# Reordering the expert matmuls by term, and moving result copies, stores, the final norm and the opening, in a two-layer backbone on one core

## The chip, the cores and the metric

The kernel runs on one NeuronCore of a Trainium2 chip. The metric is device time in microseconds (us) of one execution; the value shown is the median of 3 runs.

## The reference

A two-layer diffusion backbone over 256 latent tokens and 256 context tokens, model width 1024. The part that the change touches is the start of layer 0 (a modulated norm) and the expert part of layer 1:

```python
h_lat = modulate(rms_norm(x, norm_g[layer, 0]), sh_m, sc_m)      # shift and scale from silu(c) @ ada_w + ada_b
...
def moe_swiglu(h, w_router, b_router, w_gate, w_up, w_down):
    logits = (h @ w_router + b_router).astype(jnp.float32)
    top_v, top_i = lax.top_k(logits, TOP_K)                      # 2 of 8 experts
    weights = jax.nn.softmax(top_v, axis=-1)
    ...
    for e in range(N_EXPERTS):
        y = y + combine[..., e:e + 1] * swiglu(h, w_gate[e], w_up[e], w_down[e])   # 1024 -> 3584 -> 1024
...
return rms_norm(x, final_g)
```

## The kernel before

**Split products.** Every large product is made in three matmuls. A float32 operand is split into a high part (rounded) and a low part (the rest). `mm3` (L218) then issues high x high (L219), high x low or low x high (L220, L221) into the same accumulator. Weights come from memory as blocks of 128 x 2048 float32, 1 MB each: SP's queue loads a block (`load`, L164), ScalarE makes the high part `wh` (L181), VectorE the low part `wl` (L182). `unit` hands the next split block to TensorE and sends ahead up to 8 loads and, from the first expert on, 4 splits. The order of the blocks is a list (`_sequence`).

**Queues.** Each engine executes its instructions in order; a layer below the kernel decides the order in which an engine's instructions stand, and adds the waits. DMAs issued by SP and ScalarE share eight completion slots in rotation: an issue waits until the earlier DMA of its slot has landed.

**Opening.** x is loaded in four parts, and its squares are summed (`stats_add`, ScalarE and VectorE). TensorE sums over partitions (L359). VectorE takes the inverse root in nine short steps (`rsqrt`, L340 to L351), and TensorE spreads it by four transposes (L388). The modulation is a product of silu(c) with ada_w. Its first columns come in four groups (`ada_first(q)`, L314), each of two 1 MB blocks, 16 matmuls a block, which show as 32 pieces or fewer in a trace row. ScalarE copies the group (L317), TensorE transposes it (L319), VectorE adds the bias. Then x is multiplied (L434) and modulated (`affine_split`, L406 to L408), and the first projection starts (L219 to L221, `mm<-wh,hx`).

**Experts.** 8 experts, each at most 128 token slots, in 7 chunks of 512 hidden columns. A chunk has six units (weight blocks): two of the gate `mg`, two of up `mu`, two of down `md` for the chunk before. `half` (L1066) issues 12 matmuls for a gate or up block, accumulators `mm`; `expert_out` (L1094) issues 12 for a down block, into two accumulators `ys` (`pss`), one for each half of the output columns. `turn` (L1087) transposes the chunk's hidden values (L1090) and splits them (`ahi` by ScalarE, `alo` by VectorE). After the last chunk of experts 0 to 6, `keep_rows` copies both accumulators to buffers `yh` and `yl` on ScalarE (L1135) and stores them to `yrow` from ScalarE's queue (L1136). In the last expert the weights of the final norm, `fg`, are loaded into the same two buffers (L1246), rows of `yrow` are gathered by POOL (L1175), and `combine` (L1183) weighs and adds them on VectorE, spread over TensorE's steps (`background`).

**End.** The last expert's output is scattered (L1124, L1126), `norm_parts` squares and sums (L1273) and multiplies by the norm's weights. Then every engine reads the largest slot count and branches (L1280, L1281): the block behind it, for experts with more than 128 tokens, is not entered with these inputs. Behind the branch stand the final inverse root (L1299, `rsqrt`), the scaling (L1304, L1306) and the four stores (L1307).

Of the kernel before, what the change touches and what calls it, by code (L numbers as in the profile page):

```python
# [29 lines left out]
LOADX = 8  # L30
WIDTHS = (4, 2, 4, 4, 4, 4)
LEAD = 3
NA_ORDER = (4, 3, 0, 1, 2)
NA_FILL = (0, 0, 2, 2, 2, 2, 2, 2, 2, 2)
FFN_FILL = (3, 3, 3, 3, 2, 2)
# [76 lines left out]
def _program(tc, A, out):  # L112
# [32 lines left out]
    def small(shape, dt=F32, tag="sm", bufs=4):  # L145
        pool = smallp if tag in ("rs_v", "rs_y", "rs_t", "fss", "fs2") else wp
        return pool.tile(shape, dt, tag=tag, name=nm(tag), bufs=bufs)
# [70 lines left out]
    def mm3(ps, lh, ll, rh, rl, start, stop):  # L218
        pe.matmul(ps, lhsT=lh, rhs=rh, start=start, stop=False)  # L219
        pe.matmul(ps, lhsT=lh, rhs=rl, start=False, stop=False)  # L220
        pe.matmul(ps, lhsT=ll, rhs=rh, start=False, stop=stop)  # L221

    def put_split(hi, lo, src):
        return (act.activation(hi, src, AF.Copy),  # L224
# [129 lines left out]
    def stats_begin(nk, nt):  # L354
        return {"nk": nk, "nt": nt, "acc": None, "ps": None}
# [26 lines left out]
    def stats_end(st, d, rs=None):  # L382
        nt = st["nt"]
        if rs is None:
            rs = stats_rstd(st, d)
        bc = ps_s()
        for tt in range(nt):
            pe.transpose(bc[:, tt * P:tt * P + P], rs[:, tt:tt + 1].to_broadcast([P, P]), ident)  # L388
        return bc
# [26 lines left out]
                                     ALU.mult, ALU.add)  # L416


    st = stats_begin(KD, 4)
    for k in range(KD):  # L420
        stats_add(st, x[:, k, :], k)
    ada_first(0, ps_mm)
    bc = stats_end(st, 1024)

    gp = newpool("gp", 1)
    tn = gp.tile([P, 2, 4, 512], F32, tag="ug", name="tn")
# [631 lines left out]
    def step():  # L1058
        if background and next(background[0], True):
            background.pop(0)  # L1060
# [5 lines left out]
    def half(e, c, name, xg, ps, tag):  # L1066
        for h in range(2):
            wh, wl = unit(name, e, c, h, *tag)
            for kk in range(4):
                k = 4 * h + kk  # L1070
                mm3(ps, xg[:, k, 0, :], xg[:, k, 1, :], wh[:, 512 * kk:512 * kk + 512],
                    wl[:, 512 * kk:512 * kk + 512], k == 0, k == 7)
                if kk % SP == SP - 1:
                    step()

    def expert_in(e, c, xg, mid, *tag):
        pg = ps_mm()
        half(e, c, "mg", xg, pg, tag)
        a = mop.tile([P, 512], F32, tag="a", name=nm("a"))
        act.activation(a, pg, AF.Silu)  # L1080
        mid()
        pu = ps_mm()
        half(e, c, "mu", xg, pu, tag)
        last_mult[0] = vec.tensor_tensor(a, a, pu, ALU.mult)
        return a

    def turn(stt):  # L1087
# [7 lines left out]
    def expert_out(e, c, stt, ys, *tag):  # L1095
        last = e == NE - 1 and c == NCH - 1 and not tag
        for h in range(2):
            wh, wl = unit("md", e, c, h, *tag)
            jn = [(j, n) for j in range(2) for n in range(2)]
            jn.sort(key=lambda t: t[1])  # L1100
            for j, n in jn:
                f = 2 * h + j
                w0 = 1024 * j + 512 * n
                mm3(ys[n], stt["hi"][:, f * P:f * P + P], stt["lo"][:, f * P:f * P + P], wh[:, w0:w0 + 512],
                    wl[:, w0:w0 + 512], c == 0 and f == 0, c == NCH - 1 and f == 3)

    def slots_T(S):
        pt = ps_t()
# [23 lines left out]
    def keep_rows(e, ys):  # L1132
        for n in range(2):
            yv = mop.tile([P, 512], F32, tag=("yh", "yl")[n], name=nm("yv"), bufs=1)
            act.activation(yv, ys[n], AF.Copy)  # L1135
            nc.scalar.dma_start(yrow[e * P:e * P + P, 512 * n:512 * n + 512], yv)  # L1136

    def row_numbers():
        sm = lambda t, w=8: mop1.tile([P, 2, w] if w > 1 else [P, 2], F32, tag=t, name=nm(t))
# [36 lines left out]
                                         bass.IndirectOffsetOnAxis(ap=ri[:, 0:1], axis=0))  # L1176

    fetched = []
    last_mult = [None]

    def combine(tt):
        yy = fetched[tt]
        for n in range(2):  # L1183
            h_ = slice(512 * n, 512 * n + 512)
            a, b = yy[:, 0, h_], yy[:, 1, h_]
            with tc.issue_after(last_mult[0].ins):
                vec.tensor_scalar(a, a, rows[0][1][:, tt:tt + 1], None, ALU.mult)
            vec.scalar_tensor_tensor(a, b, rows[1][1][:, tt:tt + 1], a, ALU.mult, ALU.add)
            yield
            vec.tensor_tensor(a, a, gf[:, h_], ALU.mult)  # L1190
            vec.tensor_tensor(acc[:, tt, h_], acc[:, tt, h_], a, ALU.add)
            yield
# [78 lines left out]
    def norm_parts():  # L1271
        for n, tt, h_ in halves:
            act.activation(ps_t(), acc[:, tt, h_], AF.Square, accum_out=ss[:, tt, n:n + 1])  # L1273
            if n == 0:
                vec.tensor_tensor(o[:, tt, h_], acc[:, tt, h_], fg[n], ALU.mult)

    norm_parts()


    nmax = nc.values_load(cnt[0:1, 8:9], min_val=0, max_val=2 * P)  # L1280
    with tc.If(nmax > P):  # L1281
        for e in range(NE):
            n_e = nc.values_load(cnt[0:1, e:e + 1], min_val=0, max_val=2 * P)
            with tc.If(n_e > P):
                po2 = mop1.tile([P, 2, 8], F32, tag="po2", name=nm("po2"))
                vec.tensor_scalar(po2, pos, -float(P), None, ALU.add)
                xo, so, g = gather(po2, e)
                drain(g)
                ys = [ps_s(), ps_s()]
                for c in range(NCH):  # L1290
                    stt = {"a": expert_in(e, c, xo, lambda: None, "o")}
                    turn(stt)
                    expert_out(e, c, stt, ys, "o")
                scatter_now(e, ys, slots_T(so[0]))
        norm_parts()


    s2 = small([P, 2], tag="fs2", bufs=1)
    vec.tensor_tensor(s2, ss[:, :, 0], ss[:, :, 1], ALU.add)  # L1299
    rs = rsqrt(s2, 2, 1.0 / 1024)  # L1300
    for n, tt, h_ in halves:
        r = rs[:, tt:tt + 1]
        if n == 0:
            act.activation(o[:, tt, h_], o[:, tt, h_], AF.Identity, scale=r)  # L1304
        else:
            vec.scalar_tensor_tensor(o[:, tt, h_], acc[:, tt, h_], r, fg[n], ALU.mult, ALU.mult)  # L1306
        (nc.sync if n else nc.scalar).dma_start(out[0, tt * P:tt * P + P, h_], o[:, tt, h_])  # L1307
    xrp.release()
    mop.release()
    mop1.release()  # L1310
# [130 lines left out]
```

## Time and profile before

| | |
|---|---|
| median of 3 runs | 1835.57 us (1835.47 to 1837.29) |
| the profiled execution's own time | 1834.27 us |
| its span, first to last instruction | 1832.2 us |
| TensorE busy (PE) | 1773.5 us, 97% |
| VectorE busy (DVE) | 1332.0 us, 73% |
| ScalarE busy (ACT) | 1012.3 us, 55% |
| mean granted TensorE clock | 0.991 |
| read from memory | 476.13 MB, 263 GB/s over the span |

PE is TensorE's matmul row, PEld its weight loads (beside it), POOL is GpSimd, SP the load queue. A matmul's time in a row includes its way through the array, so the spacing of starts tells the stream's speed. "q" behind an engine marks its queue's DMA issues.

### The profile page before, as it was taken

The page shows a single profiled execution, that of the slowest core. Times are in us where ns is not written, and L with a number is a line of the kernel's source. Part 1 is how long each engine was busy: PE and PEld are TensorE (multiplying, and loading weights), DVE is VectorE, ACT ScalarE, POOL GpSimd, SP SyncE. Part 2 cuts the span into 40 slices and gives each one's busy share as a digit, 9 for nine tenths or more (in the row PEclk, how much of TensorE's full clock was granted, in tenths as well). Part 3 has the DMA queues.
Part 4 walks back from the last instruction along what each step waited for, and adds up shares of the span by engine and source line. Part 5 has one row for each costly group of instructions (what it writes and reads, how often), then busy time and mean ns, then how long its engine had stood idle before and what let it go on. Part 6 is the DMA issues. An engine that isn't in the chain of part 4 may idle for free. (4 is left out here: it accounts for less than half of the span.)

```text
span 1832.2 us, 21637 instructions
## 1 busy us (share of the span) xinstructions
PE 1773.5 (97%) x8548; PEld 1408.9 (77%) x8548; DVE 1332.0 (73%) x1413; ACT 1012.3 (55%) x1031; POOL 20.4 (1%) x19
## 2 busy tenths in 40 slices
PE   6999998999999999999999999999999999999996
PEld 4775477888888878588888878878878788788774
DVE  5632745564455578758988888888888888888797
ACT  3323634232222245746777766766766767776664
POOL 0000000000000000000000000000000000000010
PEclk9999998999999999999999999999999999999998
DMA  9567321464254317037999979989989899898990
GB/s 367 186 231 266 133 97 58 149 207 140 101 196 138 124 58 218 24 139 279 380 403 369 392 290 397 397 318 419 385 332 419 313 404 396 321 418 330 365 414 26
DMA packets 72606, 485.49 MB, mean 265 GB/s; under 512 B 7984, under 2 KB 8624, under 8 KB 16944
## 3 DMA queue, kind: packets, MB, share of 16 engines
q1 hardware_dynamic: 66416, 469.27, 66.4%
q10 hardware_dynamic: 4176, 7.94, 1.2%
q0 software_dynamic: 1904, 6.82, 1.0%
q8 instruction: 69, 1.13, 0.3%
q14 instruction: 41, 0.34, 0.0%
HBM read 476.13 MB, written 5.77 MB: 263 GB/s over the span
## 5 line engine op out<-in xcount | busy, mean ns | idle before, releaser
L182 DVE TENSOR_TENSOR wl<-raw,wh 128x2048 fp32r<-128x2048 f32 (+1 forms) x461 | 899.3, 1983 | 221.9 <-ACT wh L181 220.3
L181 ACT ACTIVATE wh<-raw 128x2048 fp32r<-128x2048 f32 (+1 forms) x461 | 745.5, 1664 | 304.6 <-PE mm L220 166.8
L220 PE MATMUL mm<-wl,xg 128*128 128x512 f32 x896 | 353.4, 394 | 11.9 <-DVE wl L182 11.9
L219 PE MATMUL mm<-wh,xg 128*128 128x512 f32 x896 | 350.6, 391 | 0.0
L221 PE MATMUL mm<-wh,xg 128*128 128x512 f32 x896 | 349.1, 390 | 0.0
L220 PEld LDWEIGHTS mm<-wl,xg 128*128 128x128 f32 x896 | 168.3, 188 | 53.9 <-DVE wl L182 20.7
L219 PEld LDWEIGHTS mm<-wh,xg 128*128 128x128 f32 x896 | 168.2, 188 | 35.1
L219 PE MATMUL mm<-hx,wh 128*128 128x512 f32 (+1 forms) x496 | 191.3, 390 | 3.8 <-ACT hx L406 3.8
L221 PEld LDWEIGHTS mm<-wh,xg 128*128 128x128 f32 x896 | 168.3, 188 | 33.8
L220 PE MATMUL mm<-hx,wh 128*128 128x512 f32 (+1 forms) x496 | 192.1, 387 | 0.0
L221 PE MATMUL mm<-hx,wl 128*128 128x512 f32 (+1 forms) x496 | 191.9, 387 | 0.0
L220 PE MATMUL pss<-wl,ahi 128*128 128x512 f32 x448 | 179.6, 401 | 2.7 <-DVE wl L182 2.7
L221 PE MATMUL pss<-wh,alo 128*128 128x512 f32 x448 | 175.2, 392 | 0.3 <-DVE alo L225 0.3
L219 PE MATMUL pss<-wh,ahi 128*128 128x512 f32 x448 | 161.4, 392 | 1.4 <-ACT wh L181 0.7
L219 PEld LDWEIGHTS mm<-hx,wh 128*128 128x128 f32 x496 | 94.0, 190 | 26.2 <-ACT hx L406 4.5
L220 PEld LDWEIGHTS mm<-hx,wh 128*128 128x128 f32 x496 | 94.3, 190 | 18.8
L221 PEld LDWEIGHTS mm<-hx,wl 128*128 128x128 f32 x496 | 94.0, 190 | 18.7
L224 ACT ACTIVATE ahi<-pst 128x512 fp32r<-128x512 f32 x56 | 33.4, 597 | 130.8 <-PE pst L1090 130.8
L220 PEld LDWEIGHTS pss<-wl,ahi 128*128 128x128 f32 x448 | 84.6, 189 | 20.1 <-DVE wl L182 4.0
L219 PEld LDWEIGHTS pss<-wh,ahi 128*128 128x128 f32 x448 | 84.2, 188 | 19.8 <-ACT wh L181 1.1
L221 PEld LDWEIGHTS pss<-wh,alo 128*128 128x128 f32 x448 | 84.7, 189 | 17.1 <-DVE alo L225 0.7
L415 DVE SCALAR_TENSOR_TENSOR x<-mm,mod,x 128x256 f32<-128x256 f32 x120 | 52.0, 478 | 39.4 <-PE mm L221 39.4
(305 smaller groups left out, 1893.6 us busy)
## 6 DMA issues: line engine op xcount, KB each, us to landing
raw<-in_mg SPq DMA_DIRECT2D x112, 1024.0 KB, 7.8
raw<-in_mu SPq DMA_DIRECT2D x112, 1024.0 KB, 8.3
raw<-in_md SPq DMA_DIRECT2D x112, 1024.0 KB, 7.9
raw<-in_ada SPq DMA_DIRECT2D x48, 1024.0 KB, 5.7
raw<-in_na_in SPq DMA_DIRECT2D x10, 1024.0 KB, 5.2
raw<-in_fg SPq DMA_DIRECT2D x10, 1024.0 KB, 5.0
raw<-in_fu SPq DMA_DIRECT2D x10, 1024.0 KB, 4.9
raw<-in_fd SPq DMA_DIRECT2D x10, 1024.0 KB, 5.0
```

The costliest lines, as they stand in the source:

```text
L181: act.activation(h_, r_, AF.Copy)
L182: vec.tensor_tensor(l_, r_, h_.bitcast(F32), ALU.subtract)
L219: pe.matmul(ps, lhsT=lh, rhs=rh, start=start, stop=False)
L220: pe.matmul(ps, lhsT=lh, rhs=rl, start=False, stop=False)
L221: pe.matmul(ps, lhsT=ll, rhs=rh, start=False, stop=stop)
L224: return (act.activation(hi, src, AF.Copy), vec.tensor_tensor(lo, src, hi.bitcast(F32), ALU.subtract))
L415: vec.scalar_tensor_tensor(x[:, db, a:b], ps[:, a:b], mod[:, l, g0 + db, c:c + 1], x[:, db, a:b], ALU.mult, ALU.add)
```

## The change

- `half` and `expert_out` issue their matmuls term by term over a block: in `half` four high x high, four with the tokens' low part, then four with the weights' low part; in `expert_out` high x high, weights' low part, hidden values' low part, for both output halves together. The last block of the program keeps the output halves apart.
- `keep_rows`: the second copy goes to VectorE, both stores to POOL's queue.
- `combine`: its first multiplication goes from VectorE to ScalarE, behind the latest Silu.
- The final norm, with its stores, becomes `final_norm`, called ahead of the branch, and again inside it.
- Opening: 30 matmuls of `ones` by `ones` come first; the spreading transposes of the inverse root are issued behind the first modulation group.

```diff
+WARM = 30
...
+    def mm3_by_term(jobs, order):
+        for i_, term in enumerate(order):
+            for ps, lh, ll, rh, rl, start, stop in jobs:
+                l_, r_ = {"hh": (lh, rh), "lh": (ll, rh), "hl": (lh, rl)}[term]
+                pe.matmul(ps, lhsT=l_, rhs=r_, start=start and i_ == 0, stop=stop and i_ == 2)
...
+    warm = ps_t()
+    for _ in range(WARM):
+        pe.matmul(warm[:, 0:P], lhsT=ones, rhs=ones, start=True, stop=True)
     st = stats_begin(KD, 4)
...
-    ada_first(0, ps_mm)
-    bc = stats_end(st, 1024)
...
+    first_stats()
+    last = ada_first(0, ps_mm)
+    rs = stats_rstd(st, 1024)
+    with tc.issue_after(last.ins):
+        bc = stats_end(st, 1024, rs)
...
-            for kk in range(4):
-                k = 4 * h + kk
-                mm3(ps, xg[:, k, 0, :], xg[:, k, 1, :], wh[:, 512 * kk:512 * kk + 512],
-                    wl[:, 512 * kk:512 * kk + 512], k == 0, k == 7)
-                if kk % SP == SP - 1:
-                    step()
+            mm3_by_term([(ps, xg[:, k, 0, :], xg[:, k, 1, :], wh[:, 512 * (k % 4):512 * (k % 4) + 512],
+                          wl[:, 512 * (k % 4):512 * (k % 4) + 512], k == 0, k == 7) for k in range(4 * h, 4 * h + 4)],
+                        ("hh", "lh", "hl"))
+            step()
...
+            if last and h == 1:
+                for n in range(2):
+                    mm3_by_term([t for t, (_, n_) in zip(jobs, jn) if n_ == n], ("hh", "hl", "lh"))
+            else:
+                mm3_by_term(jobs, ("hh", "hl", "lh"))
...
-            act.activation(yv, ys[n], AF.Copy)
-            nc.scalar.dma_start(yrow[e * P:e * P + P, 512 * n:512 * n + 512], yv)
+            if n:
+                vec.tensor_copy(yv, ys[n])
+            else:
+                act.activation(yv, ys[n], AF.Copy)
+            nc.gpsimd.dma_start(yrow[e * P:e * P + P, 512 * n:512 * n + 512], yv)
...
-            with tc.issue_after(last_mult[0].ins):
-                vec.tensor_scalar(a, a, rows[0][1][:, tt:tt + 1], None, ALU.mult)
+            with tc.issue_after(last_silu[0].ins):
+                act.activation(a, a, AF.Identity, scale=rows[0][1][:, tt:tt + 1])
...
     norm_parts()
+    final_norm()
```

TensorE's order at the start of the program, before (`raw_94`, `raw_96` are the two blocks of the first modulation group, `raw_100`, `raw_102` those of the second, `mm_237` the first projection):

```order
L359 MATMUL pss_143<-ones,w_141 128x1 x4
L388 MATMUL pss_205<-c_ident,rs_y_195 128x128
L314 MATMUL mm_152<-raw_94,c_cond 32x128 x16
L388 MATMUL pss_205<-c_ident,rs_y_195 128x128 x3
L314 MATMUL mm_152<-raw_96,c_cond 32x128 x16
L319 MATMUL pst_189<-c_ident,w_187 128x128
L314 MATMUL pss_249<-raw_100,c_cond 32x128 x16
L314 MATMUL pss_249<-raw_102,c_cond 32x128 x16
L219 MATMUL mm_237<-wh_243,hx_214 128x512
```

and now:

```order
L428 MATMUL pst_120<-ones 128x128 x30
L366 MATMUL pss_174<-ones,sacc_153 128x1 x4
L366 MATMUL pss_174<-ones,w_172 128x1 x4
L321 MATMUL mm_183<-raw_94,c_cond 32x128 x16
L321 MATMUL mm_183<-raw_96,c_cond 32x128 x16
L395 MATMUL pss_236<-c_ident,rs_y_226 128x128 x4
L326 MATMUL pst_220<-c_ident,w_218 128x128
L321 MATMUL pss_280<-raw_100,c_cond 32x128 x16
L321 MATMUL pss_280<-raw_102,c_cond 32x128 x16
L220 MATMUL mm_268<-wh_274,hx_245 128x512
```

The first group's products stand ahead of the spreading transposes; the second group's stand ahead of the first projection matmul, as before.

TensorE's order from the end of expert 6's last down block (`pss_...9`, `pss_...0` its two accumulators) into the next units, now:

```order
L228 MATMUL pss_12010<-wl_12734,ahi_12726 128x512
L228 MATMUL pss_12009<-wh_12733,alo_12727 128x512
L228 MATMUL pss_12010<-wh_12733,alo_12727 128x512
L228 MATMUL pss_12009<-wh_12733,alo_12727 128x512
L228 MATMUL pss_12010<-wh_12733,alo_12727 128x512
L228 MATMUL mm_12817<-wh_12751,xg_12169 128x512 x8
L228 MATMUL mm_12817<-wl_12752,xg_12169 128x512 x4
L228 MATMUL mm_12817<-wh_12770,xg_12169 128x512 x8
L228 MATMUL mm_12817<-wl_12771,xg_12169 128x512 x4
```

The low weights `wl` are read by the last four of a unit's twelve matmuls, and the two accumulators of a down block are finished one matmul apart.

ScalarE's order at the same place, before (`yv` the result copies, `yrow` their stores, `fg` the final norm's weights, `a` the Silu):

```order
L1135 ACTIVATE yv_12773<-pss_11978 128x512
L1136 DMA yrow<-yv_12773 128x512
L181 ACTIVATE wh_12739<-raw_12652 128x2048
L1135 ACTIVATE yv_12776<-pss_11979 128x512
L1246 DMA fg_13167<-in_fg_row 128x512
L181 ACTIVATE wh_12757<-raw_12670 128x2048
L1136 DMA yrow<-yv_12776 128x512
L181 ACTIVATE wh_12789<-raw_12700 128x2048
L1080 ACTIVATE a_12823<-mm_12786 128x512
L1246 DMA fg_13168<-in_fg_row 128x512
L181 ACTIVATE wh_12807<-raw_12718 128x2048
```

and now:

```order
L1157 ACTIVATE yv_12804<-pss_12009 128x512
L182 ACTIVATE wh_12770<-raw_12683 128x2048
L1268 DMA fg_13198<-in_fg_row 128x512
L182 ACTIVATE wh_12788<-raw_12701 128x2048
L1268 DMA fg_13199<-in_fg_row 128x512
L1094 ACTIVATE a_12854<-mm_12817 128x512
L182 ACTIVATE wh_12820<-raw_12731 128x2048
```

One copy and both stores are gone from this queue, and both loads of `fg` stand earlier; each of them waits for the store out of the buffer that it fills.

## Rows read from the trace of the kernel before

**Rows 1.** Busy by stretch (us): PE, PEld, DVE, ACT, POOL; granted clock; DMA share; GB/s.

```profile
100.00:150.00 50.00, 50.00 (x253) 37.18 (x252) 18.08 (x25) 12.24 (x16) 0.00 (x0) 1.00 0.60 219
1200.00:1250.00 50.00, 48.69 (x221) 39.57 (x220) 41.72 (x27) 34.48 (x26) 0.94 (x1) 1.00 0.84 336
1700.00:1750.00 50.00, 44.99 (x190) 35.02 (x190) 41.92 (x28) 33.83 (x23) 3.40 (x3) 0.97 1.01 409
```

**Rows 2.** Timeline, expert boundary at 1213 us, PE: start, us, what, [idle before <-releaser].

```profile
1213.30 0.39 PE L219 MATMUL mm<-wh,xg 128*128 128x512 f32 x1
1216.02 0.39 PE L219 MATMUL mm<-wh,xg 128*128 128x512 f32 x1
1217.71 0.50 PE L220 MATMUL mm<-wl,xg 128*128 128x512 f32 x1 [1.31 <-DVE wl L182]
```

**Rows 3.** Timeline, the same boundary, ACT and DVE.

```profile
1212.36 0.60 ACT L1135 ACTIVATE yv<-pss 128x512 f32<-128x512 f32 x1 [0.57 <-PE pss L221]
1213.42 1.92 ACT L181 ACTIVATE wh<-raw 128x2048 fp32r<-128x2048 f32 x1 [0.46 <-DVE alo L225]
1215.37 2.29 DVE L182 TENSOR_TENSOR wl<-raw,wh 128x2048 fp32r<-128x2048 f32 x1 [2.09 <-ACT wh L181]
```

**Rows 4.** Waits view, window 975 to 1700: total us, times, longest.

```profile
PE mm L220 <- DVE wl L182: 6.8, 5, 1.6
```

**Rows 5.** Waits view, window 1735 to 1802.

```profile
PE mm L220 <- DVE wl L182: 2.9, 6, 0.6
```

**Rows 6.** Timeline, last expert, ACT and PE.

```profile
1700.04 0.39 PE L219 MATMUL mm<-wh,xg 128*128 128x512 f32 x1
1708.25 0.36 ACTq L1246 DMA_DIRECT2D fg<-in_fg_row  x1
1708.71 5.51 ACT L181 ACTIVATE wh<-raw 128x2048 fp32r<-128x2048 f32 x3 [3.55 <-DMA yrow<-yv]
1709.58 0.39 PE L221 MATMUL mm<-wh,xg 128*128 128x512 f32 x1
1713.00 0.80 PE L220 MATMUL pss<-wl,ahi 128*128 128x512 f32 x1 [1.59 <-DVE wl L182]
1716.03 0.40 PE L219 MATMUL pss<-wh,ahi 128*128 128x512 f32 x1
```

**Rows 7.** Result stores, line L1136 (ACT queue), all 14.

```profile
DMA to landing us min/median/max: 2.0/7.4/8.4
```

**Rows 8.** Row stores of the normalized tokens, line L1008 (POOL queue), all 4.

```profile
DMA to landing us min/median/max: 4.2/4.6/5.2
```

**Rows 9.** Timeline, opening, PE.

```profile
11.84 1.86 PE L359 MATMUL pss<-ones,sacc 128*128 128x1 f32 x8 [11.84 <-DVE sacc L373]
13.56 1.84 PE L359 MATMUL pss<-ones,w 128*128 128x1 f32 x8
17.24 0.47 PE L388 MATMUL pss<-c_ident,rs_y 128*128 128x128 f32 x1 [1.83 <-DVE rs_y L351]
17.64 1.94 PE L314 MATMUL mm<-raw,c_cond 128*32 128x128 f32 x32
23.00 1.96 PE L314 MATMUL pss<-raw,c_cond 128*32 128x128 f32 x64
25.59 0.49 PE L219 MATMUL mm<-wh,hx 128*128 128x512 f32 x1 [0.64 <-ACT wh L181]
35.64 1.95 PE L314 MATMUL pss<-raw,c_cond 128*32 128x128 f32 x64
```

**Rows 10.** Opening, ACT: the first modulated block.

```profile
23.50 1.09 ACT L406 ACTIVATE hx<-tn,mod,acol 128x256 fp32r<-128x256 f32 x2 [0.88 <-DVE acol L334]
```

**Rows 11.** The load issued at 8.6 us (second block of column group 1).

```profile
DMA to landing us min/median/max: 13.5/13.5/13.5
```

**Rows 12.** Timeline, end of the program, PE, DVE and SP's queue.

```profile
1816.02 3.59 PE L1124 MATMUL mm<-a,ST 128*128 128x512 f32 x8
1824.05 0.16 DVE L1299 TENSOR_TENSOR fs<-fss 128x2 f32<-128x2 f32 x1 [2.92 <-ACTq L1281]
```

More of the change, by code (lines that the diff above doesn't have):

```diff
@@ L416, in residual, with first_stats @@
                                      ALU.mult, ALU.add)
+    warm = ps_t()
+    for _ in range(WARM):
+        pe.matmul(warm[:, 0:P], lhsT=ones, rhs=ones, start=True, stop=True)
     st = stats_begin(KD, 4)
-    for k in range(KD):
-        stats_add(st, x[:, k, :], k)
-    ada_first(0, ps_mm)
-    bc = stats_end(st, 1024)
+    def first_stats():
+        for k in range(KD):
+            stats_add(st, x[:, k, :], k)
+    first_stats()
[3 more added lines that the diff above has]
+        bc = stats_end(st, 1024, rs)
     gp = newpool("gp", 1)
@@ L1079, in expert_in @@
         a = mop.tile([P, 512], F32, tag="a", name=nm("a"))
-        act.activation(a, pg, AF.Silu)
+        last_silu[0] = act.activation(a, pg, AF.Silu)
         mid()
@@ L1083, in expert_in @@
         half(e, c, "mu", xg, pu, tag)
-        last_mult[0] = vec.tensor_tensor(a, a, pu, ALU.mult)
+        vec.tensor_tensor(a, a, pu, ALU.mult)
         return a
@@ L1099, in expert_out @@
             jn = [(j, n) for j in range(2) for n in range(2)]
-            jn.sort(key=lambda t: t[1])
+            jobs = []
             for j, n in jn:
@@ L1103, in expert_out @@
                 w0 = 1024 * j + 512 * n
-                mm3(ys[n], stt["hi"][:, f * P:f * P + P], stt["lo"][:, f * P:f * P + P], wh[:, w0:w0 + 512],
-                    wl[:, w0:w0 + 512], c == 0 and f == 0, c == NCH - 1 and f == 3)
+                jobs.append((ys[n], stt["hi"][:, f * P:f * P + P], stt["lo"][:, f * P:f * P + P], wh[:, w0:w0 + 512],
+                             wl[:, w0:w0 + 512], c == 0 and f == 0, c == NCH - 1 and f == 3))
+            if last and h == 1:
[3 more added lines that the diff above has]
+                mm3_by_term(jobs, ("hh", "hl", "lh"))
     def slots_T(S):
@@ L1178, in _program @@
     fetched = []
-    last_mult = [None]
+    last_silu = [None]
     def combine(tt):
@@ L1275, in norm_parts, with final_norm @@
                 vec.tensor_tensor(o[:, tt, h_], acc[:, tt, h_], fg[n], ALU.mult)
+    def final_norm():
+        s2 = small([P, 2], tag="fs2", bufs=1)
+        vec.tensor_tensor(s2, ss[:, :, 0], ss[:, :, 1], ALU.add)
+        rs = rsqrt(s2, 2, 1.0 / 1024)
+        for n, tt, h_ in halves:
+            r = rs[:, tt:tt + 1]
+            if n == 0:
+                act.activation(o[:, tt, h_], o[:, tt, h_], AF.Identity, scale=r)
+            else:
+                vec.scalar_tensor_tensor(o[:, tt, h_], acc[:, tt, h_], r, fg[n], ALU.mult, ALU.mult)
+            (nc.sync if n else nc.scalar).dma_start(out[0, tt * P:tt * P + P, h_], o[:, tt, h_])
     norm_parts()
+    final_norm()
     nmax = nc.values_load(cnt[0:1, 8:9], min_val=0, max_val=2 * P)
@@ L1295, in _program @@
         norm_parts()
[L1298 to L1307, printed above, removed]
+        final_norm()
     xrp.release()
```

## The prediction

> **What bounds the kernel now.** I read the view of busy time by stretch first. TensorE is busy for the whole of nearly every stretch: 50.00 of 50 us at 100 us, 48.69 in an ordinary stretch of the expert stage, 44.99 where the last expert begins [rows 1]. VectorE (41.7 us of 50) and ScalarE (34.5) come behind it, and the DMA engines move 336 to 409 GB/s. So the time is TensorE's: the number of its matmuls, which the change does not touch (30 small ones apart), times their spacing, plus its stops. Next the timeline of an expert boundary gives the spacing. From 1213.30 to 1216.02 stand twelve matmuls, so 0.227 us each [rows 2]. The 4,032 matmuls of the expert stage (56 chunks, 72 each) need 914 us at that spacing, half of the program. What can be won there is the stops, not the stream.
>
> The stops have one form. Each unit's first matmul takes the high part of the weights, the second the low part, which VectorE makes after ScalarE has made the high one. At the boundary the first starts at 1216.02 and the second only at 1217.71, after 1.31 us of idle put down to VectorE's line L182 [rows 2]. Between the starts lie 1.69 us instead of 0.23, so 1.46 us are lost. The cause is on ScalarE: the result copy (0.60 us) and the issue of its store stand ahead of the split that starts at 1213.42; VectorE's half begins at 1215.37 and takes 2.29 us [rows 3]. The waits view shows this five times between 975 and 1700 us, 6.8 us in all [rows 4]; the sixth, of the last expert, lies at 1700. Six shorter ones of the same kind, 2.9 us, lie at 1735 to 1802 [rows 5], where VectorE also combines the stored rows.
>
> **The opening new order.** Now statistics run on TensorE from 11.84 to 15.40 (two groups of 1.86 and 1.84 us). The inverse root follows on VectorE until 17.2, then a transpose, then the modulation products, so that the first modulated block starts at 23.50 and the first projection matmul at 25.59 [rows 9, 10]. The half-rate clock is in these rows: 32 pieces of a modulation product take 1.94 us at 17.64, and 64 pieces take 1.96 us at 23.00 [rows 9], the 1.2 and the 2.4 GHz level. The change puts 30 idle matmuls before and the 2 x 32 pieces into the time of the inverse root. An eight-piece group of 512 columns takes 3.59 us, two pieces to a full-precision matmul [rows 12], so one of 128 columns takes about 0.22 us at 2.4 GHz and 0.45 at 1.2. Thirty take 6.7 to 13.5 us from about 1 us on. At worst they end at 14.5 and hold the statistics back by 2.7 us; I take 9 to 11.5, since the clock should rise on the way.
>
> Two ends for the gain. If TensorE is at half rate again for all that follows, the statistics end at 15.4, the products at 19.3, four transposes and the two short VectorE steps at 21.4: 2.1 us earlier than 23.50. If the clock stays full, they end at 13.6, the products at 15.6, and the block starts at 17.2, 6.3 us earlier. But TensorE's queue has the next group's two weight blocks ahead of the first projection matmul, and the second, issued at 8.6, lands 13.5 us later, at 22.1 [rows 11]. So the projections start at 23.1 at the soonest; their first 24 matmuls take 5.5 us and end at 28.6, where they now end at 35.64 [rows 9]. That is 7.0 us. I take 4.5, the middle of 2.1 and 7.0, for nothing says how long the clock lasts over the small statistics matmuls. After 45 us TensorE is busy without a break until 200 (50.00 of 50 us in the stretch shown [rows 1]), so it is kept.
>
> **Term by term, and the copies.** With all high-weight products first, the low weights are wanted eight matmuls into a unit, 1.8 us after its first, instead of one. Against that, the second half of the output product now alternates its two accumulators, so the first result is complete 0.23 us before the end instead of 1.36 us before it. Put on the boundary: the copy starts at 1213.25, ScalarE's split at 1213.85 (no issue, no second copy), the low half ends at 1218.1, and it is wanted at 1217.85. So 0.3 us of the 1.46 stays: 1.15 us won, six times, **6.9 us**. The bounds are 0 and 8.8. The second copy, on VectorE, is priced like ScalarE's, 0.60 us [rows 3]; it waits for the end of the output product with only a transposed block's split behind it, which TensorE wants 5 us later, so it costs nothing while VectorE keeps its idle 8 us in 50.
>
> The six combine stops lose 2.9 us of idle and about 0.1 us per restart (1.46 against 1.31 above): **3.5 us**, all won, since none is longer than the 1.6 us by which the need moves; four VectorE passes go to ScalarE besides, priced 0.60 each there. Bounds 2 and 3.8. Moving the stores off ScalarE's queue also frees the loads, which share its completion slots; no TensorE stop is put down to a load, so that is worth nothing.
>
> **The last expert.** The final norm's weights (fg) are loaded into the two buffers that the last stored rows used. ScalarE's order now has the first of these loads one split behind the copy, and its issue waits until the store has landed. Before, a like wait (3.55 us on ScalarE) made TensorE lose, from 1709.58 to 1716.03, 6.45 us less ten matmuls, 4.2 us, part of it at half rate [rows 6]. Now: the unit before starts twelve matmuls ahead of 1700.04 [rows 6], at 1697.3, so the copy ends at 1697.9; a store through POOL lands after 4.2 to 5.2 us [rows 8], one under full load after up to 8.4 [rows 7], so at 1702.1 to 1706.3. Issue and split add 2.3, and TensorE wants those weights one unit (2.7 us) and the left-over 0.3 behind 1700.04, at 1703.1. It loses 1.3 to 5.5 us, up to 1.6 more if the clock falls. I take 4.2, as before: **nothing won**, between -2.9 and +2.9. Only a page speaks of POOL's own delay: the Trainium skill, SBUF — State Buffer, section "SBUF: two separate sides", says that GpSimd cannot write its transfer descriptors while certain VectorE operations hold a shared port, and advises the ACT or SP queue. An estimate by that page, with one VectorE pass of 2.29 us as the delay, makes the sum 2.3 us smaller.
>
> **The end.** VectorE's first step of the final norm waits 2.92 us at the branch, until 1824.05 [rows 12]. Ahead of the branch it starts as the last square is done, and the branch then runs beside the stores. **2.6 us**; bounds 0 (the branch follows the landing) and 2.9.
>
> **Sum.** 4.5 + 6.9 + 3.5 + 0 + 2.6 = 17.5 us, off the profiled execution's 1834.27 us (span 1832.2): 1816.8. The median of the runs is 1.3 us above that execution, so 1818.
>
> **Rivals.**
> - Weak side: the opening stays at half rate (2.1) and the last expert loses 2.9. The gain is 12.2: 1823. For it: the granted clock falls where TensorE stops, 0.97 in the stretch of the last expert [rows 1]. Chance 0.18.
> - Strong side: opening 6.3, boundaries 8.8, last expert +2.9. The gain is 24.1: 1811. Chance 0.15.
> - The change does not do what it says: VectorE, busy 83 to 84% in the stage [rows 1], paces it, and a removed stop returns a unit later. Then 10.4 us go: 1828. Against it: between 975 and 1700 us TensorE waits for low weights five times only [rows 4], once in some 50 units. Chance 0.08.
> - Slower: the output products now write two accumulators in turn, 1,344 matmuls, and the stream loses its clock or spacing. At half rate a matmul costs 0.23 us more (the doubling of rows 9); 77 of them eat the gain, and a fifth (269) adds 62 us: 1880. Against it: in this kernel too the pairs change accumulators in each block, with the clock at 1.00 [rows 1]. The Trainium skill, TensorE: Matmul & The Clock Gate, section "A second HAM failure mode: psum-queue depth-cycling", tells of a kernel that cycled through accumulators and lost its clock so; this trace does not agree yet. Chance 0.04.
>
> **Numbers.** My forecast keeps 0.53; 0.02 is for what I did not think of. The range 1810 to 1826 holds it with its bounds, nearly all of the weak and the strong side, and leaves out the other two. A measurement tells 0.2% (3.7 us) from no change. Forecast, weak, strong and most of the third are faster: 0.91. No change, 0.05, is the third with a poor opening or end; slower 0.04.
>
> **What would show it.** Right: no idle on VectorE at boundaries, or under 0.5 us; the first modulated block before 21.4; the norm's first step at once after the last square; one ScalarE wait of 3 to 6 us on a store at the last expert. Wrong: matmul spacing above 0.227 in the expert stage, a granted clock under 1.00 in its middle, or VectorE without idle and TensorE waiting for high weights.

## The result, and the profile after

The changed kernel takes 1855.76 us (median of 4 runs, 1853.25 to 1857.98), the kernel before 1836.43 (1835.47 to 1837.38). The ratio is 1.0105, with a 95% interval of 1.0087 to 1.0122: **slower by 1%**, where 1818 was forecast. The profiled execution took 1857.98 us, its span is 1856.2.

Where it went is read by looking up the same instruction in both traces and taking the difference of its starts. The experts are counted from 0 to 7:

| place (us in the kernel before) | shift, after minus before |
|---|---|
| 50 to 220, opening done | -2.8 |
| 698 to 830, ahead of the experts | -1.9 |
| 1041 to 1058, in expert 1 | +0.9 |
| 1697, TensorE starts expert 7 | +25.6 |
| 1816, last expert's output scattered | +24.2 |
| 1824, first step of the final norm | +21.5 |
| end of the span | +24.0 |

Nearly all of it, 24.7 us, comes between 1058 and 1697, in the regular stream of experts 2 to 6, where the forecast had five boundaries' gain and nothing else.

The view of busy time by stretch, in the columns of [rows 1], of the changed kernel:

```profile
1200.00:1250.00 50.00, 49.31 (x219) 38.74 (x217) 41.08 (x26) 34.96 (x25) 2.10 (x3) 1.00 0.98 370
1300.00:1350.00 50.00, 49.06 (x215) 38.26 (x214) 41.67 (x24) 34.76 (x24) 1.10 (x2) 1.00 0.96 351
1700.00:1750.00 50.00, 49.14 (x215) 38.43 (x216) 41.72 (x26) 33.09 (x26) 4.84 (x4) 1.00 0.90 350
```

In the same windows TensorE is busier than before (49.31 against 48.69 us at 1200, 49.14 against 44.99 at 1700 [rows 1]) and the clock is granted in full, yet at 1300 it gets through only 215 matmuls in 50 us. A stretch of the kernel before without a boundary has 228:

```profile
1400.00:1450.00 50.00, 50.00 (x228) 41.41 (x227) 43.66 (x25) 35.65 (x25) 0.00 (x0) 1.00 0.99 386
```

The busy share hides the loss: a matmul is recorded for 0.39 us while the next starts 0.227 us behind it, so a stop of a few tenths disappears in it. The waits view of TensorE from 975 to 1700 us hides it too. It shows many short waits, 7.2 us in all, against the 24.7 that the stretch lost; the 1.6 us stops of [rows 4] are gone from it:

```profile
PE mm L228 <- DVE wl L183: 5.5, 25, 0.2
PE pss L228 <- DVE wl L183: 1.7, 5, 0.3
```

What shows the loss is ScalarE's timeline, 1306 to 1335 us, one and a half chunks (start, us, what, idle before):

```profile
1308.67 0.60 ACT L231 ACTIVATE ahi<-pst 128x512 fp32r<-128x512 f32 x1 [2.68 <-PE pst L1104]
1309.16 3.71 ACT L182 ACTIVATE wh<-raw 128x2048 fp32r<-128x2048 f32 x2
1315.95 0.60 ACT L1094 ACTIVATE a<-mm 128x512 f32<-128x512 f32 x1 [3.07 <-PE mm L228]
1316.44 7.31 ACT L182 ACTIVATE wh<-raw 128x2048 fp32r<-128x2048 f32 x4
1326.47 0.60 ACT L231 ACTIVATE ahi<-pst 128x512 fp32r<-128x512 f32 x1 [2.72 <-PE pst L1104]
1326.96 3.71 ACT L182 ACTIVATE wh<-raw 128x2048 fp32r<-128x2048 f32 x2
```

A chunk takes 17.80 us (1308.67 to 1326.47). ScalarE makes two splits between the transposed block `ahi` and the Silu `a`, and four behind the Silu. In the kernel before it was three and three, and a chunk took 16.79 (1306.35 to 1323.14):

```profile
1306.35 0.60 ACT L1080 ACTIVATE a<-mm 128x512 f32<-128x512 f32 x1 [1.72 <-PE mm L221]
1306.84 5.51 ACT L181 ACTIVATE wh<-raw 128x2048 fp32r<-128x2048 f32 x3
1315.40 0.60 ACT L224 ACTIVATE ahi<-pst 128x512 fp32r<-128x512 f32 x1 [3.04 <-PE pst L1090]
1315.89 5.52 ACT L181 ACTIVATE wh<-raw 128x2048 fp32r<-128x2048 f32 x3
1323.14 0.60 ACT L1080 ACTIVATE a<-mm 128x512 f32<-128x512 f32 x1 [1.72 <-PE mm L221]
```

So one split has moved behind the Silu, and the Silu waits 3.07 us for the end of the gate product. The timeline of TensorE and VectorE in the next chunk shows what that does:

```profile
1333.75 0.60 ACT L1094 ACTIVATE a<-mm 128x512 f32<-128x512 f32 x1 [3.08 <-PE mm L228]
1334.25 7.31 ACT L182 ACTIVATE wh<-raw 128x2048 fp32r<-128x2048 f32 x4
1336.19 4.49 DVE L183 TENSOR_TENSOR wl<-raw,wh 128x2048 fp32r<-128x2048 f32 x2 [2.79 <-ACT wh L182]
1336.27 2.04 PE L228 MATMUL mm<-wh,xg 128*128 128x512 f32 x8
1338.54 1.20 PE L228 MATMUL mm<-wl,xg 128*128 128x512 f32 x4 [0.22 <-DVE wl L183]
1339.57 1.07 PE L228 MATMUL pss<-wh,ahi 128*128 128x512 f32 x4
1340.74 1.19 PE L228 MATMUL pss<-wl,ahi 128*128 128x512 f32 x4
```

The first split behind the Silu is that of mu1, the second up block, which TensorE begins at 1336.27. Its low half is done at 1338.48 (1336.19 and one pass of 2.29 us, [rows 3]), because Silu, high half and low half follow each other. TensorE needs it at 1338.15: the eight matmuls on the high half end at 1338.31, the last of them started 0.39 earlier, and the next is due 0.23 behind that start. It starts at 1338.54, and the one behind it follows after 0.34 us instead of 0.227 (the four take 1.20 us in all, where four in the stream take 1.07). VectorE's next low half is then late for the down block as well (1340.74, where the four matmuls ahead began at 1339.57). Together that is 1 us a chunk.

### The profile page after: what moved, and what is told of

It reads as the page before. It is cut to its first block, busy times and chain, and to the rows that moved or that the text cites. A ratio compares the mean times of both kernels' runs of the same rounds, so it can differ in the third digit from the quotient of the medians.

```text
span 1856.2 us, 21775 instructions
## 1 busy us (share of the span) xinstructions
PE 1804.1 (97%) x8608; PEld 1411.3 (76%) x8608; DVE 1328.9 (72%) x1416; ACT 1007.8 (54%) x1028; POOL 29.7 (2%) x33
## 3 DMA queue, kind: packets, MB, share of 16 engines
q8 instruction: 70, 1.15, 0.3%
## 4 chain that ended last, share of the span: by engine, by line
PE 67%; DVE 12%; DMA 9%; issue 6%; ACT 5%; ACTq 0%; DVEq 0%
PE mm L228 13%; PE mm L220 11%; PE mm L221 11%; PE mm L222 11%; PE pss L228 11%; DVE wl L183 10%; DMA raw<-in_md 5%; ACT wh L182 4%; DMA raw<-in_mg 2%; PE mm L872 1%; PE pss L881 1%; PE pst L1104 1%; PE pss L650 1%; PE mm L634 1%; PE pss L275 1%
## 5 line engine op out<-in xcount | busy, mean ns | idle before, releaser
L228 PE MATMUL mm<-wh,xg 128*128 128x512 f32 x1792 | 447.5, 392 | 1.3 <-ACT wh L182 1.2
L228 PEld LDWEIGHTS mm<-wh,xg 128*128 128x128 f32 x1792 | 332.5, 188 | 76.4 <-ACT wh L182 8.7
L228 PE MATMUL mm<-wl,xg 128*128 128x512 f32 x896 | 247.0, 397 | 9.1 <-DVE wl L183 8.8
L228 PEld LDWEIGHTS mm<-wl,xg 128*128 128x128 f32 x896 | 163.4, 188 | 58.8 <-DVE wl L183 28.0
L228 PE MATMUL pss<-wl,ahi 128*128 128x512 f32 x448 | 130.1, 412 | 9.0 <-DVE wl L183 5.9
L228 PE MATMUL pss<-wh,alo 128*128 128x512 f32 x448 | 120.9, 391 | 0.0
L228 PE MATMUL pss<-wh,ahi 128*128 128x512 f32 x448 | 120.7, 391 | 0.0
L221 PEld LDWEIGHTS mm<-hx,wh 128*128 128x128 f32 x496 | 94.4, 190 | 18.8
L222 PEld LDWEIGHTS mm<-hx,wl 128*128 128x128 f32 x496 | 94.1, 190 | 18.8
L228 PEld LDWEIGHTS pss<-wl,ahi 128*128 128x128 f32 x448 | 77.6, 188 | 39.7 <-DVE wl L183 27.4
L1094 ACT ACTIVATE a<-mm 128x512 f32<-128x512 f32 x56 | 33.3, 594 | 130.1 <-PE mm L228 130.1
L222 PE MATMUL mm<-ah,wl 128*128 128x512 f32 x176 | 68.5, 389 | 0.0
```

Of the source, the lines that this page charges most:

```text
L228: pe.matmul(ps, lhsT=l_, rhs=r_, start=start and i_ == 0, stop=stop and i_ == 2)
L1094: last_silu[0] = act.activation(a, pg, AF.Silu)
```

## The experiments

Theory A: the order on ScalarE's queue is the cause. Theory B: output products that alternate two accumulators slow the stream. Theory C: the loads pace it, which the chain of waits of the changed kernel suggests, since it leads through `raw<-in_md`:

```profile
PE mm L228 13%; PE mm L220 11%; PE mm L221 11%; PE mm L222 11%; PE pss L228 11%; DVE wl L183 10%; DMA raw<-in_md 5%; ACT wh L182 4%; DMA raw<-in_mg 2%; PE mm L872 1%; PE pss L881 1%; PE pst L1104 1%; PE pss L650 1%; PE mm L634 1%; PE pss L275 1%
```

All runs, with the ratio to the kernel before on the same chip:

| run | us, median | ratio, 95% interval |
|---|---|---|
| changed kernel | 1855.8 | 1.0105 (1.0087 to 1.0122) |
| e1 Silu behind the mu1 split | 1826.3 | 0.9949 (0.9930 to 0.9968) |
| e2 Silu behind the md0 split | 1820.7 | 0.9918 (0.9901 to 0.9934) |
| e3 term order undone | 1817.9 | 0.9904 (0.9886 to 0.9922) |
| e4 undone in gate and up blocks | 1821.9 | 0.9921 (0.9904 to 0.9938) |
| e5 undone in down blocks | 1880.1 | 1.0244 (1.0227 to 1.0261) |
| e7 e3 with the order disturbed | 1896.7 | 1.0328 (1.0311 to 1.0346) |
| e8 copies and stores alone | 1826.6 | 0.9951 (0.9935 to 0.9968) |
| e9 e3, term order in two units | 1813.1 | 0.9871 (0.9855 to 0.9888) |
| e10 e9 without idle matmuls | 1813.2 | 0.9880 (0.9864 to 0.9897) |
| e11 e9, opening undone | 1818.2 | 0.9902 (0.9885 to 0.9918) |
| e12 e9, combine undone | 1816.9 | 0.9900 (0.9883 to 0.9916) |
| e13 e9, norm behind the branch | 1812.4 | 0.9869 (0.9853 to 0.9885) |

### e1 and e2: the Silu held back

```diff
-        last_silu[0] = act.activation(a, pg, AF.Silu)
+        with tc.issue_after(wh_at[0].ins):     # e1: the mu1 split; e2 has last_wh[0], the md0 split
+            last_silu[0] = act.activation(a, pg, AF.Silu)
```

> The changed kernel with one more order edge: ScalarE's Silu of a chunk is issued behind the split of the second up block (mu1), as it stands in the kernel before; nothing else. Theory A (queue order): in the changed kernel the mu1 split stands behind the Silu, which waits for the end of the gate product; from there Silu 0.50 to the next start, high half 1.91, low half 2.3, with hand-overs 4.95 us, against 2.72 + 1.81 = 4.53 us until TensorE wants it, so each chunk loses about 1 us (17.77 instead of 16.79). With the edge the chunks return to 16.79 and the time to 1815 to 1822. Theory B (two accumulators in turn slow the stream): TensorE's order is unchanged, the time stays 1850 to 1860. Theory C (the loads pace it, as the chain of waits names them): the time stays within 3 us of the changed kernel's 1855.8.

> The same edge one split further: the Silu behind the split of the first down block (md0), so two splits earlier than in the changed kernel. Theory A: the first split behind the Silu now serves the unit after next but one, 2.7 us more room, so no more stop than in e1: within 3 us of it, 1812 to 1822, and if the 0.7 us to spare in e1 is eaten somewhere, faster than e1 by 2 to 5 us. A price is possible on the other side: a Silu that waits for a split comes later, but what it feeds is wanted two units on. Theories B and C: as the changed kernel, 1850 to 1860.

Measured: 1826.3 and 1820.7. In e1's timeline of ScalarE there are three splits on either side of the Silu again, and the chunk is 16.80 us (1304.49 to 1321.29):

```profile
1304.49 0.60 ACT L1098 ACTIVATE a<-mm 128x512 f32<-128x512 f32 x1 [1.27 <-PE mm L230]
1304.99 5.51 ACT L182 ACTIVATE wh<-raw 128x2048 fp32r<-128x2048 f32 x3
1314.00 0.60 ACT L233 ACTIVATE ahi<-pst 128x512 fp32r<-128x512 f32 x1 [3.50 <-PE pst L1108]
1314.50 5.51 ACT L182 ACTIVATE wh<-raw 128x2048 fp32r<-128x2048 f32 x3
1321.29 0.60 ACT L1098 ACTIVATE a<-mm 128x512 f32<-128x512 f32 x1 [1.28 <-PE mm L230]
```

One edge on one queue gives back 29.4 us, and a second step 5.7 more. TensorE's order of instructions is that of the changed kernel, in e2 to the end and in e1 up to the last expert. That rules out B and C as the main cause. In e2 the stretch from 1300 to 1350 us holds 226 matmuls, with more bytes per second from the same loads:

```profile
1300.00:1350.00 50.00, 49.94 (x226) 41.05 (x225) 43.71 (x26) 35.57 (x26) 1.10 (x2) 1.00 0.98 378
```

e1 misses its range by 4 us in the last expert. TensorE waits there four times, up to 1.5 us, for low halves of a down block; e2 has none of these waits:

```profile
PE pss L230 <- DVE wl L183: 3.8, 4, 1.5
```

The traces show what differs there. In e1 the layer below has split the four transposes of a chunk's hidden block in three chunks of the last expert, with 7.5 us between the pairs in the first of them; `ahi` waits for the second pair, the split behind `ahi` comes late, and so does the low half of the down block:

```profile
1726.45 0.38 PE L1108 MATMUL pst<-c_ident,a 128*128 128x128 f32 x2
1733.95 0.38 PE L1108 MATMUL pst<-c_ident,a 128*128 128x128 f32 x2
1734.36 0.60 ACT L233 ACTIVATE ahi<-pst 128x512 fp32r<-128x512 f32 x1 [5.93 <-PE pst L1108]
1742.73 1.20 PE L230 MATMUL pss<-wl,ahi 128*128 128x512 f32 x4 [1.49 <-DVE wl L183]
```

In e2 the four stand together, as in the changed kernel:

```profile
1725.08 0.60 PE L1106 MATMUL pst<-c_ident,a 128*128 128x128 f32 x4
```

### e3, e4, e5: the term order undone, in all blocks or in some

```diff
-            mm3_by_term([(ps, xg[:, k, 0, :], ...
+            for kk in range(4):
+                k = 4 * h + kk
+                mm3(ps, xg[:, k, 0, :], xg[:, k, 1, :], ...      # e3, e4: half; e3, e5: expert_out
```

> The changed kernel with the matmuls of gate, up and down blocks interleaved again as before; opening, copies, stores, combine and final norm stay changed. ScalarE's order is then that of before (three splits between Silu and the transposed block, three behind it). Theory A: no stop per chunk, but the six boundary stops are there, at 0.9 to 1.5 us each; left of the gain are the opening (1.9 to 2.8 us by the trace), the end (2.7) and what copies, stores and combine bring (0 to 4): 1826 to 1832. Theory B gives the same range, since the accumulators no longer alternate. Theory C (loads disturbed by POOL's stores): the stores are still on POOL, so it stays at 1845 to 1856.

Measured: 1817.9, better than expected by 8 us. The stops at the boundaries are smaller than I had taken them, 0.90 us each (1.13 between two starts instead of 0.23, where the kernel before had 1.70), and the last expert gains more (below). With the stores still on POOL there is no loss, against C. e3 also shows that the term order is worth little over a whole expert: e2 and e3 both take 120.3 us for each of experts 2 to 5 (from its first gate matmul to that of the next), the kernel before 121.0 to 121.3.

> Only the gate and up blocks are interleaved again; the down blocks stay term by term with two accumulators in turn. ScalarE's order keeps the mu1 split behind the Silu. Theory A: the low half of mu1 is wanted one matmul into its unit, so the room is 2.72 + 0.23 = 2.95 us against the 4.95 us of the chain: 2.0 us per chunk and what the refill adds, over about 42 chunks 84 us on the 1816 to 1822 of e1: 1895 to 1925. Theory B: the down blocks are as in the changed kernel, so 1850 to 1860. Theory C: 1850 to 1860.

Measured: 1821.9, far outside the range of A. The premise was wrong, not the theory. I had counted two splits between `ahi` and Silu and taken that for the changed kernel's order. In e4 it is `ahi` that has moved by one, and the split behind the Silu is md0's, as in the kernel before:

```
L1096 ACTIVATE a1985_10945<-mm1978_10908 128x512
L182 ACTIVATE wh1983_10929<-raw1969_10853 128x2048
```

The block `wh1983` is read by the accumulators of a down block. From here on I went by what each split serves. Theory B, which wanted 1850 to 1860 from the down blocks alone, falls.

> The changed kernel with the down blocks interleaved as before (one accumulator finished in front of the other); gate and up blocks stay term by term. ScalarE's order, read by what each split serves, keeps the mu1 split behind the Silu in the chunks from the second expert on. Theory A (queue order): the loss stays. The low half of md0 is now wanted 0.5 us earlier still, so rather more: 1850 to 1890. Theory B (two accumulators in turn slow the stream): the alternation is gone, 1815 to 1825. Theory C (loads): 1850 to 1860.

Measured: 1880.1, inside the range of A, 24 us slower than the changed kernel, though the accumulators no longer alternate. The term order of gate and up blocks alone brings the harmful queue order, and the interleaved down block wants its low half sooner. TensorE's waits from 975 to 1700 us:

```profile
PE pss L221 <- DVE wl L183: 24.8, 34, 1.3
PE mm L228 <- DVE wl L183: 5.2, 24, 0.2
```

### e7: the queue order alone

The look-ahead of splits is cut by one unit at mg0 and by two at mg1, and the splits traced at mu0 get an edge behind the Silu. All matmuls stay interleaved.

```diff
+            fewer[0] = 1 + h if name == "mg" and late(e, c) and not tag else 0
...
-            for inst in hold:
+            for inst in hold + behind:     # behind: the chunk's Silu
                 es.enter_context(tc.issue_after(inst.ins))
```

> The kernel e3 (matmuls interleaved as before, the rest of the change kept) with ScalarE's order alone disturbed: in the 39 chunks from the third expert's first (and up to the fourth of the last expert) the splits of mu1 and what follows are issued behind the Silu. TensorE's order is that of e3. This is the test that e4 should have been: there the split behind the Silu was md0's, which I had counted wrongly. Theory A: the low half of mu1 is wanted 2.72 + 0.23 = 2.95 us behind the end of the gate product and comes after 4.95: 2.0 us and up to 0.4 of refill per chunk, 39 chunks, 78 to 94 us on e3's 1817.9: 1896 to 1912. Theory B: TensorE's order is that of a kernel without loss: 1815 to 1822. Theory C: the stores are as in e3: 1815 to 1822.

Measured: 1896.7, 78.8 us above e3, at the lower end of A's range; B and C wanted 1822 at most. Regular chunks take 18.8 us. The layer below the kernel answered by drawing a down block's first matmul ahead of the late low half, so the wait shows at that matmul, and TensorE's order is not quite e3's as I had written:

```profile
PE pss L220 <- ACT wh L182: 42.8, 33, 1.4
```

So the term order does not cause the loss by itself; without it nearly the same queue order costs about twice as much per chunk (2.0 us against 1.0). Nearly, because in e7 `ahi` also stands one split later than in the changed kernel; it does so in e4 too, where a regular chunk takes 16.85 us, so that costs 0.06. The term order is both the trigger and a partial remedy.

### e8: copies and stores alone

```diff
             yv = mop.tile([P, 512], F32, tag=("yh", "yl")[n], name=nm("yv"), bufs=1)
-            act.activation(yv, ys[n], AF.Copy)
-            nc.scalar.dma_start(yrow[...], yv)
+            if n:
+                vec.tensor_copy(yv, ys[n])
+            else:
+                act.activation(yv, ys[n], AF.Copy)
+            nc.gpsimd.dma_start(yrow[...], yv)
```

> The kernel before with one part of the change: the second result copy on VectorE, both stores from POOL's queue. Theory A, by the shifts between the traces of before and e3: 0.61 to 0.65 us at each of six boundaries (3.8) and 4.2 in the last expert, where the norm's weights no longer wait 3.55 us for a store: 8 us, 1825 to 1831 against 1836. Rival D: at the boundary it is the term order that matters (as I had forecast), and the copies change nothing: 1832 to 1837. Rival E: the last expert's gain came with the combine step, not the stores: 1830 to 1834.

Measured: 1826.6, 9.8 us below the kernel before. This part is a gain by itself, at the boundaries (six waits, 4.4 us in all, where [rows 4] have five with 6.8) and in the last expert, where ScalarE's wait for the store (3.55 us in [rows 6]) is 1.3 in the waits view of 1690 to 1730 us:

```profile
ACT wh L181 <- DMA yrow<-yv: 1.3, 1, 1.3
```

### e9: the term order only where it is wanted

```diff
+            if (name, h) in (("mg", 1), ("mu", 0)) and c == 1 and e > 0 and not tag:
+                mm3_by_term([...], ("hh", "lh", "hl"))
+                step()
+                continue
             for kk in range(4):
...
+        with tc.issue_after(wh_at[0].ins):
+            last_silu[0] = act.activation(a, pg, AF.Silu)
```

> The kernel e3, with term order only in the two units per expert that stand behind the result copies (second gate block and first up block of chunk 1), and the Silu held behind the mu1 split, so that ScalarE's order stays that of before. Theory A: e3's boundary stop, 1.13 instead of 0.23 between two matmuls, goes in six places and does not return, since VectorE's next low halves (1215.21 and 1217.41 in e3) come before they are wanted (1216.5 and 1217.9): 5.4 us, 1811 to 1814 against e3's 1817.9. Rival: the stop returns one or two units later, 1816 to 1819.

Measured: 1813.1, as expected of A; faster than both kernels. From 975 to 1700 us one wait is left, three units behind the last boundary, and an expert takes 119.3 us:

```profile
PE mm L223 <- DVE wl L183: 0.7, 1, 0.7
```

The edge on the Silu is part of it: in the program without the edge, the mu1 split stands behind the Silu in chunk 1 of experts 2 to 7, just where mg1 goes term by term. That program was not timed.

### e10 to e13: the small parts, each undone from e9

e10 sets `WARM = 0`; e11 restores the opening, e12 combine's multiplication on VectorE, e13 the place of the final norm, each as in the kernel before.

> The kernel e9 without the 30 idle matmuls at the start; the rest of the new opening stays. Theory F (the idle matmuls raise the clock and pay): statistics and products run at half rate again, the statistics end near 15.4 and the first modulated block starts near 21.3 instead of 18.55; what of that reaches the projections is up to 2 us, so 1813 to 1816 against e9's 1813.1 and 0.985 to 0.989 of the kernel before. Rival G (they pay nothing, because the second modulation group waits for its load until 20.8 in e9 anyway): 1811 to 1814, the first projection matmul within 0.5 us of 25.05.

> The kernel e9 with the opening of before, in order and without idle matmuls. The shift between the traces of before and e3 was 3.9 us at 200 us and 4.2 at 800; between before and the changed kernel it was 2.8 and 1.95. So the opening is worth 2 to 4.2 us: 1815 to 1817.5. If the opening is worth nothing in the end (given back where the clock falls at 224 to 290 and 654 us): 1812 to 1814.

> The kernel e9 with combine's first multiplication on VectorE again, behind the chunk's product. By my forecast the six stops at 1735 to 1802 us of the kernel before, 3.5 us, come back: 1816 to 1817.5. Rival: they went with the matmuls' or copies' order and not with this step, or ScalarE's four passes cost as much elsewhere: 1812 to 1814.5.

> The kernel e9 with the final norm and its stores behind the branch again, as before. My forecast gave its move 2.6 us: then this is 1815 to 1817 against e9's 1813.1, and from the last square's end to the end of the span it takes 2.6 us longer. Theory H, by the traces of before and of the changed kernel: the norm starts 2.7 us earlier, but the stores land 1.2 us later behind their issue and the closing instructions then take 1.2 us more, so from the last square's end to the end it is 10.65 against 10.85 us: 1812.5 to 1814, and the tail in the trace within 0.5 us of e9's.

Measured: 1813.2, 1818.2, 1816.9, 1812.4 against e9's 1813.1. Theory F falls: the idle matmuls pay nothing. The opening's order is worth 5.1 us by the medians (the intervals of the two ratios overlap a little; the profiled executions differ by 4.0). Combine's part is worth 3.8, and its six waits are back in e12's view of 1700 to 1800 us, while e9 has none of them:

```profile
PE mm L223 <- DVE wl L183: 2.8, 6, 0.6
```

The place of the final norm is worth nothing. In e13 the norm starts 3.00 us late as before, and the span still ends 10.8 us behind the last square, against 10.6 in e9.

## Why the prediction was wrong

**The step that failed** is in the part "Term by term, and the copies". It asked when the low weights are wanted, and put that on the boundary alone. That ScalarE and VectorE make them in the same order as before was taken for granted, everywhere else in the stage, and the regular chunks were priced at nothing. But the layer that decides the order answered the new matmul order with a new ScalarE order, 42 chunks long, from expert 2 to the end. The order's own price is e1's 29.4 us, or e2's 35.1. The rows were there: in ScalarE's order printed ahead of the prediction, three splits (`wh_12739`, `wh_12757`, `wh_12789`) stand between copy and Silu before, and two now; `wh_12820`, behind the Silu, is the same block as `wh_12789`, which stood ahead of it. I read these rows for copies and loads only.

**The rival that came nearest** was "the change does not do what it says", with 0.08 and a price of 10.4 us. I argued against it from the five waits in [rows 4]. Those were the waits of the old queue order, and say nothing about the new one. The rival on the slower side, accumulators in turn, was the wrong mechanism (e4, e5). Of the signs set for being wrong, a matmul spacing above 0.227 us did show, but only behind stops, and the clock stayed at 1.00.

**The other terms.**
- Opening, 4.5 forecast: -2.8 at 220 us and -1.9 at 830 in the changed kernel, -3.9 and -4.2 at the same places in e3; 5.1 us in the runs of e11. Kernels with this same opening scatter there: -3.0 in e9, -4.2 in e12 at 50 to 220. The order was right, but the part given to the clock was not: e10 loses nothing without the idle matmuls, so that 4.5 came near is in part luck. The limit was the load, as said, but TensorE's timeline of the changed kernel has it later than I did: the second block of the second group was awaited until 23.22 (I had 22.1), its 32 pieces took 1.93 us at half rate (I had 1.0), and the first projection matmul came at 25.09 instead of 23.1.

```profile
20.83 1.08 PE L321 MATMUL pss<-raw,c_cond 128*32 128x128 f32 x32 [1.44 <-DMA raw<-in_ada]
23.22 1.93 PE L321 MATMUL pss<-raw,c_cond 128*32 128x128 f32 x32 [1.31 <-DMA raw<-in_ada]
25.09 0.80 PE L220 MATMUL mm<-wh,hx 128*128 128x512 f32 x1
```

- Boundaries, 6.9 forecast (1.15 each), bound 8.8: put down to the wrong part. With the queue order mended, e2 takes 17.15 us for the chunk at the boundary to expert 3, where the kernel before took 18.51, but 17.94 and 18.03 for its second and fourth, which took 17.57 and 17.75. An expert gains 0.7 us, and the copies alone bring as much (e8, 120.3 us an expert): they took 0.56 to 0.85 us off each stop (at the first, 1.67 between two starts became 1.11). Only e9, with term order in two units, takes the rest, 1.7 us an expert. One figure of the working was off without harm: in the kernel before the first result was complete 1.13 us before the end of the product, not 1.36, and the copy's start at 1213.25 goes with 1.13.
- Combine, 3.5 forecast: 3.8 in e12.
- Last expert, nothing forecast, bound +2.9: the gain exceeds it (e8 wins 3.3 us between 1711 and 1731 us of the kernel before). The price of POOL's store was mis-sized. I had 4.2 to 8.4 us to landing; in the place that matters the first store was issued at 1723.82 and landed at 1726.16, 2.3 us, and ScalarE lost 1.34 there:

```profile
1726.67 1.92 ACT L182 ACTIVATE wh<-raw 128x2048 fp32r<-128x2048 f32 x1 [1.34 <-DMA yrow<-yv]
```

Over all 14 stores the landing is no faster than from ScalarE's queue [rows 7]:

```profile
DMA to landing us min/median/max: 2.3/7.3/8.8
```

The estimate by the Trainium skill's warning on stores through GpSimd (SBUF — State Buffer, "SBUF: two separate sides") would have made the sum smaller by 2.3 us; no run here shows such a delay in the last expert.

- End, 2.6 forecast: the norm's first step does start at once (0.25 us of idle, where it was 2.92 [rows 12]). But the four stores land 3.2 to 4.7 us behind their issue instead of 2.7 to 3.5, and what follows the last landing (1853.71) up to the end of the span takes 2.5 us instead of 1.2. From the end of the last square to the end of the span it was 10.8 us and is 10.6. My bound of 0 ("the branch follows the landing") was the right value: SP's semaphore steps of the branch now stand behind that landing, where they used to be done before the norm began. VectorE's first step:

```profile
1845.58 0.16 DVE L1301 TENSOR_TENSOR fs<-fss 128x2 f32<-128x2 f32 x1 [0.25 <-ACT pst L1295]
```

The line of the output stores, and SP's line of the branch:

```profile
DMA to landing us min/median/max: 3.2/3.9/4.7
L1316 SPq EVENT_SEMAPHORE  x9: 17/17/17, 1853.9 to 1854.5; - x9
```

The difference of 41 us between forecast (1816.8) and profiled execution splits so, by the table of shifts: 30.5 in experts 2 to 6 (24.7 lost, 5.8 not won), 2.8 in experts 0 and 1, 2.6 in the opening, 3.2 in the last expert, 2.4 at the end. For expert 0 the trace shows stops of 1.56 us at 855.93, where TensorE waits for VectorE's product, and of 1.50 us at 865.12 and at 873.38, where it waits for low halves; no run took them apart.

**Open.** Why the layer below chooses another queue order for gate and up blocks that go term by term was not looked into; e4, e5 and the program of e9 without the edge only show that these blocks decide it. Nor was it looked into why the edge of e1 splits the transposes in the last expert and that of e2 does not.

## What to carry to other kernels

When a scheduler sets the queues, a change of order on one engine is a change of order on all. Compare, for each engine, which block each preparing step serves and what it stands behind, over a whole period of the loop and not only at the place that the change aims at. Then price the chain from what it waits for to its use. And do not trust a high busy share or a short list of waits where an engine is pipelined: count what it gets through in a stretch.

## What the runs showed of the hardware that was not expected

The idle matmuls raised the clock, but not where the opening's time is decided. In the changed kernel their pieces start 0.21 us apart until 5.3 us and 0.11 us apart from then on, full rate. The clock granted behind them is half in the statistics and half again when the first projections run (the column behind POOL's):

```profile
12.50:19.00 6.50, 6.50 (x79) 5.87 (x80) 1.47 (x9) 0.28 (x1) 0.00 (x0) 0.50 1.02 423
23.00:29.00 6.00, 5.78 (x42) 4.42 (x43) 5.54 (x12) 2.64 (x6) 0.00 (x0) 0.50 1.01 421
```

In e9 the statistics do find full rate (8 pieces in 1.05 us, 1.86 in [rows 9]). But the second group then waits for its load, and it and the first projections run at half rate:

```profile
11.97 1.05 PE L368 MATMUL pss<-ones,sacc 128*128 128x1 f32 x8 [2.09 <-DVE sacc L382]
20.79 1.94 PE L323 MATMUL pss<-raw,c_cond 128*32 128x128 f32 x32 [3.05 <-DMA raw<-in_ada]
25.05 0.80 PE L222 MATMUL mm<-wh,hx 128*128 128x512 f32 x1
```

In e10, without them, TensorE's timeline has the first group's 64 pieces at half rate (3.64 us, as in the sum), but the second group's last block, which has to wait for its load, meets full rate, and the first projection matmul comes at 23.36 instead of 25.05:

```profile
15.47 3.64 PE L323 MATMUL mm<-raw,c_cond 128*32 128x128 f32 x64
22.35 1.08 PE L323 MATMUL pss<-raw,c_cond 128*32 128x128 f32 x32 [0.51 <-DMA raw<-in_ada]
23.36 0.50 PE L222 MATMUL mm<-wh,hx 128*128 128x512 f32 x1
```

What came earlier in e9 ended in a wait for the load, and what followed the load ran slower; e9 and e10 take the same time.

Short stops cost more than their wait. After each of the 30 recorded between 975 and 1697 us, the second matmul started 0.34 us behind the first instead of 0.227, and the next ones 0.23 to 0.24; 7.2 us of recorded waits went with 24.7 us lost.
